# Layer 1's modulation beside the first mixer's attention, the second mixer's q products between the two norms, and roots with PSUM operands

## The chip, the cores and the metric

The kernel runs on one core of a Trainium2 chip. Its engines are TensorE (PE in the profile; PEld is its weight load), VectorE (DVE), ScalarE (ACT), GpSimd (POOL) and SyncE (SP), which issues most DMAs. The metric is the device time of one execution in microseconds, as the median of several runs.

## The reference

A two-layer diffusion trunk over 256 latent and 256 context tokens with D = 1024, in float32. Each layer takes six modulation vectors for each stream (latent and context) from a condition vector, runs a mixer and then a mixture of experts.

```python
for l in range(DEPTH):                       # two layers
    ml = split((silu(c)     @ ada_w[l] + ada_b[l]), 6)   # latent stream
    mc = split( silu(c_ctx) @ ada_w[l] + ada_b[l],  6)   # context stream
    nl = rmsnorm(hl, norm1_g[l]) * (1 + ml[1]) + ml[0]
    nc = rmsnorm(hc, norm1_g[l]) * (1 + mc[1]) + mc[0]
    if l % 2 == 0: yl, yc = conv_diffattn_mixer(nl, nc, ...)   # mixer 0
    else:          yl, yc = bigla_mixer(nl, nc, ...)           # mixer 1
    hl = hl + ml[2] * yl
    nl = rmsnorm(hl, norm2_g[l]) * (1 + ml[4]) + ml[3]
    y  = hier_moe(nl [and nc], ...)          # 32 experts, top 2 in the top group
    hl = hl + ml[5] * y                      # and hc likewise in layer 0
```

Mixer 0 is a convolution beside a differential attention (4 heads, two softmax maps each) with one joint output projection. Mixer 1 is a gated linear attention in both directions: products q, k, v and g of the normalized tokens, and a decay `log_sigmoid(a1 @ w_a2 + b_a2) / 16` from a low-rank gate.

## The kernel before

The program has four stages one after the other: mixer 0, MoE 0, mixer 1, MoE 1. The streams live in `H`, 128 tokens by 1024, blocks 0 and 1 latent, 2 and 3 context. Products in full precision are made of three (`mm3`): both operands are split into a rounded half `h` (by ScalarE) and the rest `l` (by GpSimd or VectorE), and PE takes h·h, h·l and l·h. `quarter` splits a quarter of a 1 MB weight tile so, on L371 (`wh`) and L372 (`wl`). Weight tiles come from one ring, `wt`, of four 1 MB buffers, and are loaded on SP's queue. The program is written in plain order; a scheduler then picks the order of each engine's instructions by a modelled time, so that a row's place on an engine is not that of its line. Every engine runs its own list strictly in order.

**Modulation.** `ada_steps(l, r)` computes the r-th pair of modulation vectors of layer l (r = 0: shift and scale of the first norm, 1: gate of the mixer and shift of the second, 2: the rest). It is a generator of eight steps; a step loads 1 MB of `ada_w` (L196) and multiplies it in four short products (L201). After the eighth it adds the bias (L210), for r other than 1 applies the norm's gain (L214), and for r other than 0 writes the rows to DRAM on GpSimd's queue. `ada_cols(1)` (L267) transposes (1,0) into columns for mixer 1.

**Mixer 0.** `attn_block(b, fill)` runs the attention of one block of 128 queries, four heads: QK products (L614), softmax, transposes of p (L634), P·V (L640), and calls `fill` after every head. For the latent blocks `fill_lat` makes one step of (1,0), eight in all; the four loads of w_out follow. For the context blocks `fill_ctx` makes a piece of `out_lat`, the latent half of the output projection: 96 products into `pj`, closed by `yt` (L710), from which the latent norm, route and modulate of MoE 0 start. The context half follows after the last block.

**Mixer 1.** It loads constants, sets `wf` to zero (L820) and loads the gate's weights into it by ten small loads (L823 to L827). `norm_mod_T` normalizes one stream: sums of squares (L325), reciprocal roots by an integer guess and two Newton steps (`rstd_of`, L280 to L286), `xn` (L328, L329), transposes (L335), then shift and scale into `xa` (L340) and its split into XH and XL (L341, L342). The code normalizes both streams, with the steps of (1,1) as filler whose tiles are mixer 1's own buffers, not yet in use (`S`, `sg`, `bT`, `attb`). Then come the gate: split weights `wv` (L879, L880) and `wa2h`, `wa2l` (L874, L875), products a1 and z (L895), and the decay L by Abs, Exp and Ln (L896 to L900). The q products (`lat_T`, L870) are written after it, then k, then the levels of the linear attention on VectorE, and the V projection, with (1,2) as filler.

Of the kernel before, what the change touches and what calls it, by code (L numbers as in the profile page):

```python
# [9 lines left out]
FT = mybir.dt.float32  # L10
FR = mybir.dt.float32r
BF = mybir.dt.bfloat16
I32 = mybir.dt.int32
U32 = mybir.dt.uint32
AF = mybir.ActivationFunctionType
# [4 lines left out]
D = 1024  # L20
# [60 lines left out]
def trunk_kernel(ctx: ExitStack, tc: tile.TileContext, A: dict, out: bass.AP):  # L81
# [7 lines left out]
    def pool(es, name, side):  # L89
        return es.enter_context(tc.tile_pool(name=name, bufs=1, side=side, reuse_waits="tile"))  # L90

    def pj(dt=FT):
        return psum.tile([128, 512], dt, name="pj", tag="pj", bufs=4)
# [6 lines left out]
    def wk(dt=FT):  # L100
        return wkp[0].tile([128, 512], dt, name="wk", tag="wk", bufs=2)
# [5 lines left out]
    def trps(dt=FT):  # L107
        return psum.tile([128, 512], dt, name="trps", tag="tr", bufs=2)
# [94 lines left out]
    def ada_steps(l, r, mpool, pool=None):  # L203

        m, bias, gn = ada_open(l, r, mpool)
        ps = trps() if (l, r) == (1, 2) else wk()
        for k in range(8):
            ada_k(ps, ada_tile(l, r, k, pool), k)
            if k == 7:
                nc.vector.tensor_add(m, bias, ps)  # L210
                if r != 1:
                    o = 64 if r == 0 else 0
                    v = m[o:o + 64]
                    nc.vector.scalar_tensor_tensor(v, v, 1.0, gn[o:o + 64], op0=OP.add, op1=OP.mult)  # L214
                if r:

                    ns = 2 - l
                    d = dram.tile([2, ns, D], FT, name=f"row{l}{r}", tag=f"row{l}{r}")
                    for h in range(2):
                        nc.gpsimd.dma_start(d[h].rearrange("s (g c) -> g s c", g=2), m[64 * h:64 * h + 64:16 * (2 // ns)])  # L220
                    rows[l, r] = d
            yield
# [39 lines left out]
    def ada_cols(l):  # L262

        t = const.tile([128, 2, 2, 4, 2], FT, name=f"cols{l}", tag=f"cols{l}")
        ps = trps()
        for i in range(4):
            nc.tensor.transpose(ps[:, i * 128:(i + 1) * 128], mods[l, 0][:, i * 128:(i + 1) * 128], ident)  # L267
        v = ps.rearrange("p (i g s r) -> p i g s r", i=4, g=4, s=2)[:, :, :, :, 0]
        for g in range(4):
            nc.vector.tensor_copy(t[:, g // 2, g % 2], v[:, :, g])  # L270
        return t.rearrange("p w g i s -> p w (g i) s")

    def rstd_of(dst, ss, n, pool, temps=None):

        c = 0.703952253
        k2 = (0.5 * c ** 3) ** 2
        sh = list(ss.shape)
        tag = f"rsq{sh[-1]}"
        w, t = temps or [pool.tile(sh, FT, name="rs" + i, tag=tag + i, bufs=2) for i in "wt"]
        nc.vector.tensor_scalar(w, ss, 1.0 / (n * k2), EPS / k2, op0=OP.mult, op1=OP.add)  # L280
        nc.vector.tensor_scalar(dst.bitcast(I32), w.bitcast(I32), 1, None, op0=OP.logical_shift_right)
        nc.vector.tensor_scalar(dst.bitcast(I32), dst.bitcast(I32), -1.0, float(0x5F1FFFF9), op0=OP.mult, op1=OP.add)
        for a in (2.38924456, 3 / c ** 2):
            nc.vector.tensor_mul(t, dst, dst)
            nc.vector.tensor_mul(t, t, w)
            nc.vector.scalar_tensor_tensor(dst, t, -a, dst, op0=OP.add, op1=OP.mult)  # L286

    def mm3(ps, st, mv, k0, k1):

        (sh, sl), (mh, ml) = st, mv  # L290
        nc.tensor.matmul(ps, sh, mh, start=k0, stop=False)  # L291
        nc.tensor.matmul(ps, sh, ml, start=False, stop=False)  # L292
        nc.tensor.matmul(ps, sl, mh, start=False, stop=k1)  # L293
# [24 lines left out]
    def norm_mod_T(pool, st, cols):  # L318

        ss = pool.tile([128, 2], FT, name="ss", tag="ss", bufs=2)  # L320
        rs = pool.tile([128, 2], FT, name="rs", tag="rs", bufs=2)
        xs = []
        for i in range(2):
            x = pool.tile([128, D], FT, name="xn", tag="xn", bufs=4)
            nc.scalar.activation(x, H[:, 2 * st + i], AF.Square, accum_out=ss[:, i:i + 1])  # L325
            xs.append(x)
        rstd_of(rs, ss, D, pool)
        nc.vector.tensor_scalar(xs[0], H[:, 2 * st], rs[:, 0:1], None, op0=OP.mult)  # L328
        nc.scalar.activation(xs[1], H[:, 2 * st + 1], AF.Copy, scale=rs[:, 1:2])  # L329
        t = slice(256 * st, 256 * st + 256)  # L330
        for kp in range(4):
            ps = trps()
            for j in range(4):
                k = 2 * kp + j // 2
                nc.tensor.transpose(ps[:, j * 128:(j + 1) * 128], xs[j % 2][:, k * 128:(k + 1) * 128], ident)  # L335
            for kk in range(2):
                k = 2 * kp + kk
                v = ps[:, kk * 256:kk * 256 + 256]
                a = pool.tile([128, 256], FT, name="xa", tag="xa", bufs=4)
                nc.vector.tensor_scalar(a, v, cols[:, 1, k, st:st + 1], cols[:, 0, k, st:st + 1], op0=OP.mult, op1=OP.add)  # L340
                nc.scalar.activation(XH[:, k, t], a, AF.Copy)  # L341
                (nc.gpsimd if kk else nc.vector).tensor_sub(XL[:, k, t], a, XH[:, k, t].bitcast(FT))  # L342
# [20 lines left out]
    def load_cols(src, pieces):  # L363
        return [load_half(src, pieces, hf) for hf in range(2)]

    def quarter(pool, ts, q, bufs, alt=False, dve=False):

        w = ts[q // 2][:, (q % 2) * 1024:(q % 2 + 1) * 1024]
        wh = pool.tile([128, 1024], FR, name="wh", tag="wsh", bufs=bufs)
        wl = pool.tile([128, 1024], FR, name="wl", tag="wsl", bufs=bufs)  # L370
        nc.scalar.activation(wh, w, AF.Copy)  # L371
        (nc.vector if dve or alt and q % 2 else nc.gpsimd).tensor_sub(wl, w, wh.bitcast(FT))  # L372
        return wh.rearrange("p (k n) -> p k n", k=2), wl.rearrange("p (k n) -> p k n", k=2)
# [25 lines left out]
    def mixer0():  # L399
        es = ExitStack()  # L400
        with es:
# [314 lines left out]
                    k = 2 * q + kk  # L716
                    mm3(ps, (ch[:, k, t], cl[:, k, t]), (w[0][:, kk], w[1][:, kk]), k == 0, k == 7)

            ad = ada_steps(1, 0, bp)
            ts = []  # L720

            def fill_lat(i):
                next(ad, None)

            def out_lat():
                for n in range(2):
# [19 lines left out]
                attn_block(b, fill_lat)  # L746
            for _ in ad:
                pass
            cols1[0] = ada_cols(1)
            ts += [load_cols(w, [(512 * n, 512)]) for n in range(2)]  # L750
            es6.close()
            es2.close()
# [31 lines left out]
    def mixer1():  # L784
        es = ExitStack()
        with es:
# [44 lines left out]
            def split2(x0, x1):  # L831

                hl = [xp.tile([128, 1024], FR, name="w" + t, tag="ws" + t, bufs=3) for t in "hl"]
                for i, x in enumerate((x0, x1)):
# [7 lines left out]
            rp = pool(es2, "raw1", "right")  # L842
            tsq = load_cols(w_in, [(0, 512)])


            free = [S.rearrange("p a h e -> p (a h e)"), sg.rearrange("p b c -> p (b c)"),
                    bT.rearrange("p a h t -> p (a h t)"), attb]

            fill = ada_steps(1, 1, mp, free[::-1])
            cols = cols1[0]  # L850
            for st in range(2):
                norm_mod_T(rp, st, cols)
            for _ in fill:
                pass
            es2.close()
            es4 = ExitStack()
            lp = pool(es4, "gl1", "right")
            L = lp.tile([128, 4, 2, 512], FT, name="L")
            vc = lp.tile([128, 2, D], FT, name="vc")

            def lat_T(w, pss, q):

                wh, wl = w
                for h in range(4):
                    for kk in range(2):
                        k = 2 * q + kk
                        o = pss[h // 2][:, 256 * (h % 2):256 * (h % 2) + 256]
                        a = slice(h * 128, (h + 1) * 128)
                        for i, (st, mv) in enumerate(((wh, xh), (wh, xl), (wl, xh))):
                            nc.tensor.matmul(o, st[:, kk, a], mv[:, k, :256], start=k == 0 and h % 2 == 0 and i == 0,  # L870
                                             stop=k == 7 and i == 2, skip_group_check=True)


            nc.scalar.activation(wa2s[0], wa2, AF.Copy)  # L874
# [25 lines left out]
                nc.vector.tensor_sub(L[:, bb[0]:bb[1] + 1], L[:, bb[0]:bb[1] + 1], E)  # L900


            pss = [pj(), pj()]
            for q in range(4):
                lat_T(quarter(xp, tsq, q, 3), pss, q)
            for i in range(2):
                nc.scalar.activation(qk[:, 0, 2 * i:2 * i + 2], pss[i].rearrange("p (h t) -> p h t", h=2), AF.Copy, scale=128 ** -0.5)
            ts = load_cols(w_in, [(512, 512)])
            pss = [pj(), pj()]
            pt = [pj(), pj()]  # L910
# [117 lines left out]
                nc.vector.tensor_copy(att[g:g + 32, :, g:g + 32], a32[g:g + 32])  # L1028


            fill = ada_steps(1, 2, mp, free[0:1])
            for n in range(2):
                _, pt = proj(xp, load_cols(w_in, [(1024 + 512 * n, 512)]), 3, toks=range(4), xh=xh, xl=xl, fill=fill)
                for i in range(2):
                    nc.scalar.activation(vc[:, i, n * 512:(n + 1) * 512], pt[2 + i], AF.Copy)
                    nc.vector.tensor_copy(V[:, i, n * 512:(n + 1) * 512], pt[i])
# [811 lines left out]
```

## Time and profile before

| | |
|---|---|
| median of 3 runs | 1535.17 us (1533.19 to 1537.72) |
| the profiled execution | 1534.12 us, span 1532.3 us, mean granted TensorE clock 0.944 |
| busy, of the span | PE 84%, PEld 43%, DVE 38%, ACT 24%, POOL 20% |
| HBM read | 495.68 MB, 324 GB/s over the span |
| MoE 0, MoE 1 | products from 357.9 us, and from about 1080 us |
| mixer 1's start | last product of MoE 0 (L1490) at 829.6 us |

The profile lists a row for each group of instructions: start, duration, engine, line, operation, output and inputs by their names (buffer numbers left out), shape; in square brackets the idle time of the engine just before it and what ended it. SPq is SP's queue of DMA issues. A row of the stretches view has the stretch, its length, the busy time and count of each engine, the granted clock, the mean busy share of the 16 DMA engines, and GB/s.

### The profile page before, as it was taken

The numbers are of one execution on the slowest core, as the hardware profiler recorded it, in microseconds if no ns is written. First come the engines' busy times: TensorE is split into PE (matmuls) and PEld (weight loads), VectorE is DVE, ScalarE is ACT, GpSimd is POOL, SyncE is SP. The second block draws the span as 40 slices with busy tenths as digits, with TensorE's granted clock in tenths as the row PEclk, the third lists the DMA queues.
The fourth block names the chain that finished last, engine by engine and source line by source line (L and its number), as shares of the span: only waits on it lengthen the run. The fifth ranks groups of instructions, "written<-read, shape, count | busy, mean of one in ns | idle before, by whom it ended". The sixth has DMA issues, their size and how long they took to land. (4 is left out here: it accounts for less than half of the span.)

```text
span 1532.3 us, 19018 instructions
## 1 busy us (share of the span) xinstructions
PE 1283.2 (84%) x7485; PEld 658.3 (43%) x7485; DVE 581.1 (38%) x1182; ACT 368.4 (24%) x700; POOL 300.5 (20%) x206
## 2 busy tenths in 40 slices
PE   5998978678789899999987999997965778767776
PEld 4665636564234345443422676675412212212211
DVE  4489895753002131231205556766202102202121
ACT  3245563451010101010102574444100000000000
POOL 1467601431001010100103443442000000000010
PEclk9999997898999999999998999998998899999989
DMA  9857261156999999999999623468799999999995
GB/s 317 287 204 256 108 220 48 68 212 277 421 422 424 422 422 423 412 422 423 423 424 357 226 92 133 166 224 352 301 427 427 426 426 427 427 427 426 427 426 250
DMA packets 100828, 498.10 MB, mean 325 GB/s; under 512 B 17605, under 2 KB 30248, under 8 KB 45948
## 3 DMA queue, kind: packets, MB, share of 16 engines
q1 hardware_dynamic: 96780, 490.37, 79.7%
q0 software_dynamic: 1680, 6.16, 1.2%
q8 instruction: 61, 1.00, 0.2%
q10 hardware_dynamic: 2272, 0.28, 0.2%
q14 instruction: 35, 0.29, 0.1%
HBM read 495.68 MB, written 1.10 MB: 324 GB/s over the span
## 5 line engine op out<-in xcount | busy, mean ns | idle before, releaser
L1553 PE MATMUL pj<-wx,xgT 128*32 128x512 f32 (+1 forms) x1496 | 313.9, 642 | 70.0 <-DMA wx<-in_moe_w_dram 70.0
L1553 PEld LDWEIGHTS pj<-wx,xgT 128*32 128x32 f32 (+1 forms) x1496 | 76.2, 120 | 256.6 <-DMA wx<-in_moe_w_dram 131.8
L1553 PE MATMUL pj<-wt,xgT 128*32 128x512 f32 (+1 forms) x704 | 160.1, 629 | 27.1 <-DMA wt<-in_moe_w_dram 23.4
L1453 DVE SCALAR_TENSOR_TENSOR s<-s,gc,pj 128x512 f32<-128x512 f32 x20 | 15.0, 748 | 428.8 <-PE pj L1553 374.4
L1562 PE MATMUL pj<-wx,hT 128*32 128x512 f32 (+1 forms) x792 | 167.4, 609 | 9.4 <-DMA wx<-in_moe_w_dram 5.3
L372 POOL TENSOR_TENSOR wl<-wt,wh 128x1024 fp32r<-128x1024 f32 x50 | 124.9, 2506 | 158.6 <-ACT wh L371 151.7
L291 PE MATMUL pj<-wh,XH 128*128 128x512 f32 x304 | 123.4, 416 | 18.8 <-ACT p L623 10.1
L292 PE MATMUL pj<-wl,XH 128*128 128x512 f32 x304 | 124.8, 410 | 1.4 <-POOL wl L372 1.4
L293 PE MATMUL pj<-wh,XL 128*128 128x512 f32 x304 | 122.8, 405 | 0.2
L1494 POOL TENSOR_TENSOR H<-H,sc 128x512 f32<-128x512 f32 x24 | 30.7, 1278 | 394.6 <-DVE sc L1493 394.6
L1481 POOL TENSOR_TENSOR H<-H,sc 128x512 f32<-128x512 f32 x16 | 20.4, 1275 | 446.3 <-DVE sc L1480 446.3
L371 ACT ACTIVATE wh<-wt 128x1024 fp32r<-128x1024 f32 x66 | 68.9, 1055 | 64.7 <-PE pj L293 44.3
L1553 PEld LDWEIGHTS pj<-wt,xgT 128*32 128x32 f32 (+1 forms) x704 | 37.9, 118 | 106.4 <-issue 59.2
L1562 PEld LDWEIGHTS pj<-wx,hT 128*32 128x32 f32 (+1 forms) x792 | 42.4, 114 | 94.1 <-issue 72.5
L291 PEld LDWEIGHTS pj<-wh,XH 128*128 128x128 f32 x304 | 58.9, 195 | 48.2 <-ACT p L623 11.6
L1452 ACT ACTIVATE s<-pj 128x512 f32<-128x512 f32 x20 | 12.0, 598 | 262.8 <-PE pj L1553 262.8
L1458 ACT ACTIVATE hT<-trps 128x512 f32<-128x512 f32 x20 | 11.9, 597 | 248.5 <-PE trps L1456 248.5
L545 DVE SCALAR_TENSOR_TENSOR wk<-hp,vt,wk 128x512 f32<-128x512 f32 x90 | 67.5, 750 | 1.7
L292 PEld LDWEIGHTS pj<-wl,XH 128*128 128x128 f32 x304 | 59.2, 195 | 17.6 <-issue 2.4
L293 PEld LDWEIGHTS pj<-wh,XL 128*128 128x128 f32 x304 | 59.1, 194 | 14.2 <-DVE XL L1096 1.3
L1562 PE MATMUL pj<-wt,hT 128*32 128x512 f32 (+1 forms) x280 | 54.6, 598 | 2.8 <-ACT hT L1458 2.8
L1388 PE MATMUL wk<-P,XH 128*128 128x256 f32 x192 | 52.2, 306 | 5.2 <-ACT xgT L1390 3.8
(468 smaller groups left out, 2020.1 us busy)
## 6 DMA issues: line engine op xcount, KB each, us to landing
wx<-in_moe_w_dram SPq DMA_DIRECT2D x266, 1024.0 KB, 19.6
wt<-in_moe_w_dram SPq DMA_DIRECT2D x107, 1024.0 KB, 19.6
wa<-in_ada_w_dram SPq DMA_DIRECT2D x16, 1024.0 KB, 4.8
wt<-in_gla_w_in_dram SPq DMA_DIRECT2D x12, 1024.0 KB, 8.0
H<-in_moe_w_dram SPq DMA_DIRECT2D x11, 1024.0 KB
S<-in_ada_w_dram SPq DMA_DIRECT2D x10, 1024.0 KB, 12.2
wt<-in_ada_w_dram SPq DMA_DIRECT2D x8, 1024.0 KB, 6.5
wt<-in_ab_w_in_dram SPq DMA_DIRECT2D x6, 1024.0 KB, 11.7
```

The lines of the kernel that those rows point to most:

```text
L291: nc.tensor.matmul(ps, sh, mh, start=k0, stop=False)
L292: nc.tensor.matmul(ps, sh, ml, start=False, stop=False)
L293: nc.tensor.matmul(ps, sl, mh, start=False, stop=k1)
L371: nc.scalar.activation(wh, w, AF.Copy)
L372: (nc.vector if dve or alt and q % 2 else nc.gpsimd).tensor_sub(wl, w, wh.bitcast(FT))
L545: e.scalar_tensor_tensor(av, hp[:, cb, :, t:t + 256], cw[:, t, cb:cb + 1], av, op0=OP.mult, op1=OP.add)
L1388: nc.tensor.matmul(ps[:, k], M['X'][h][:, k0 + k, b * 128:(b + 1) * 128], P[:, b], start=b == 0 and h == 0, stop=b == nb - 1 and h == 1)
L1453: nc.vector.scalar_tensor_tensor(s, s, gc, h3, op0=OP.mult, op1=OP.mult)
L1481: (nc.vector if hf else nc.gpsimd).tensor_add(H[:, b, c], H[:, b, c], t)
L1494: (nc.vector if hf else nc.gpsimd).tensor_add(H[:, b, c], H[:, b, c], t)
L1553: nc.tensor.matmul(ps[o:o + w], xgT[:, k, o:o + w], W[nm, x, k // 4][:, k % 4], start=k == 0, stop=k == 7)
L1562: nc.tensor.matmul(ys[hf][o:o + w], hT[:, k, o:o + w], W["2", x, k // 2][:, k % 2, hf * 512:(hf + 1) * 512], start=k == 0, stop=k == 3)
```

## The change

1. In mixer 0, a generator `early` makes the steps of (1,0), then the columns of (1,0), then the steps of (1,1) and of (1,2): 24 steps in place of 8. `fill_lat` makes three of them per head. All 24 loads use the `wt` ring.
2. In mixer 1 the filler steps and their borrowed buffers are gone.
3. In mixer 1 the q products are written between the norm of stream 0 and that of stream 1, ahead of the gate.
4. `norm_mod_T` uses a new root, `rstd_free`: its guess and its square are held in a PSUM bank (`wk`), and the square is made by ScalarE.
5. The bank of (1,2)'s sums is a `wk` one like the others.

```diff
-        ps = trps() if (l, r) == (1, 2) else wk()
+        ps = wk()
...
+    def rstd_free(dst, ss, n, pool):
+
+        c = 0.703952253
+        k2 = (0.5 * c ** 3) ** 2
+        m = ss.shape[-1]
+        w = pool.tile(list(ss.shape), FT, name="rsw", tag=f"rsq{m}w", bufs=2)
+        b = wk()
+        d0, t = b[:, 0:m], b[:, m:2 * m]
+        nc.vector.tensor_scalar(w, ss, 1.0 / (n * k2), EPS / k2, op0=OP.mult, op1=OP.add)
+        nc.vector.tensor_scalar(d0.bitcast(I32), w.bitcast(I32), 1, None, op0=OP.logical_shift_right)
+        nc.vector.tensor_scalar(dst.bitcast(I32), d0.bitcast(I32), -1.0, float(0x5F1FFFF9), op0=OP.mult, op1=OP.add)
+        for a in (2.38924456, 3 / c ** 2):
+            nc.scalar.activation(t, dst, AF.Square)
+            nc.vector.tensor_mul(t, t, w)
+            nc.vector.scalar_tensor_tensor(dst, t, -a, dst, op0=OP.add, op1=OP.mult)
...
-        rstd_of(rs, ss, D, pool)
+        rstd_free(rs, ss, D, pool)
...
-            ad = ada_steps(1, 0, bp)
+            def early():
+
+                yield from ada_steps(1, 0, bp)
+                cols1[0] = ada_cols(1)
+                for r in (1, 2):
+                    yield from ada_steps(1, r, bp)
+            ad = early()
...
             def fill_lat(i):
-                next(ad, None)
+                for _ in range(3):
+                    next(ad, None)
...
-            cols1[0] = ada_cols(1)
             ts += [load_cols(w, [(512 * n, 512)]) for n in range(2)]
...
-            free = [S.rearrange("p a h e -> p (a h e)"), sg.rearrange("p b c -> p (b c)"),
-                    bT.rearrange("p a h t -> p (a h t)"), attb]
-
-            fill = ada_steps(1, 1, mp, free[::-1])
             cols = cols1[0]
-            for st in range(2):
-                norm_mod_T(rp, st, cols)
-            for _ in fill:
-                pass
...
+            norm_mod_T(rp, 0, cols)
             def lat_T(w, pss, q):
...
+            pss = [pj(), pj()]
+            for q in range(4):
+                lat_T(quarter(xp, tsq, q, 3), pss, q)
+            for i in range(2):
+                nc.scalar.activation(qk[:, 0, 2 * i:2 * i + 2], pss[i].rearrange("p (h t) -> p h t", h=2), AF.Copy, scale=128 ** -0.5)
+            norm_mod_T(rp, 1, cols)
...
-            fill = ada_steps(1, 2, mp, free[0:1])
             for n in range(2):
-                _, pt = proj(xp, load_cols(w_in, [(1024 + 512 * n, 512)]), 3, toks=range(4), xh=xh, xl=xl, fill=fill)
+                _, pt = proj(xp, load_cols(w_in, [(1024 + 512 * n, 512)]), 3, toks=range(4), xh=xh, xl=xl)
```

The lines behind the root shift by 15 or 16, and in mixer 1 by 21 or 22: mm3 is L307 to L309, QK L630, p's transposes L650, P·V L656, `yt` L726, the squares' sums L341, `xn` L344 and L345, `xa` L356, XH L357, `wh` and `wl` L387 and L388, `wf`'s loads L845 to L849, `wa2h` L895, `wv` L900.

On PE, in mixer 0, the first product of `out_lat` (`pj_1770<-wh_...`, from w_out) before, with the eighth and last modulation step (`wt_2062`) ahead of it:

```order
L640 MATMUL wk_1772<-V_593,at_1896 128x128 x4
L201 MATMUL wk_1805<-wt_2062,st32_81 32x512 x4
L614 MATMUL pj_1768<-kT_592,qT_591 128x512
L614 MATMUL pj_1769<-kT_592,qT_591 128x512
L614 MATMUL pj_1770<-kT_592,qT_591 128x512
L614 MATMUL pj_1771<-kT_592,qT_591 128x512
L614 MATMUL pj_1768<-kT_592,qT_591 128x256 x2
L614 MATMUL pj_1769<-kT_592,qT_591 128x256 x2
L291 MATMUL pj_1770<-wh_2198,XH_75 128x512
L292 MATMUL pj_1770<-wl_2199,XH_75 128x512
```

And the same place after the change, with the last seven of the 24 steps (`wk_2089` collects (1,2)):

```order
L201 MATMUL wk_2089<-wt_2096,st32_81 32x512 x4
L201 MATMUL wk_2089<-wt_2128,st32_81 32x512 x4
L630 MATMUL pj_1768<-kT_592,qT_591 128x256 x2
L685 MATMUL trps_2219<-cst_71,o4_2195 128x128 x4
L630 MATMUL pj_1769<-kT_592,qT_591 128x256 x2
L201 MATMUL wk_2089<-wt_2134,st32_81 32x512 x4
L201 MATMUL wk_2089<-wt_2140,st32_81 32x512 x4
L201 MATMUL wk_2089<-wt_2172,st32_81 32x512 x4
L201 MATMUL wk_2089<-wt_2178,st32_81 32x512 x4
L201 MATMUL wk_2089<-wt_2184,st32_81 32x512 x4
L307 MATMUL pj_1770<-wh_2313,XH_75 128x512
```

The attention of the second latent block and QK products of the first context block, of which a part stood behind `out_lat`'s first products, now stand ahead of them, between the steps.

On ACT, at mixer 1's start before (`xn` of the two streams, XH of stream 0, then the gate's weights):

```order
L329 ACTIVATE xn_6097<-H_66,rs_6094 128x1024
L329 ACTIVATE xn_6168<-H_66,rs_6165 128x1024
L341 ACTIVATE XH_75<-xa_6117 128x256
L341 ACTIVATE XH_75<-xa_6121 128x256
L341 ACTIVATE XH_75<-xa_6130 128x256
L341 ACTIVATE XH_75<-xa_6134 128x256
L341 ACTIVATE XH_75<-xa_6143 128x256
L341 ACTIVATE XH_75<-xa_6147 128x256
L341 ACTIVATE XH_75<-xa_6156 128x256
L879 ACTIVATE wv_6291<-wf_6072 128x16x32 x2
L874 ACTIVATE wa2h_6057<-wf_6072 128x512
```

And after (`wk_6215` holds stream 0's square, `wk_6402` stream 1's):

```order
L300 ACTIVATE wk_6215<-rs_6209 128x2
L900 ACTIVATE wv_6474<-wf_6187 128x16x32 x2
L895 ACTIVATE wa2h_6172<-wf_6187 128x512
L300 ACTIVATE wk_6215<-rs_6209 128x2
L300 ACTIVATE wk_6402<-rs_6396 128x2
L345 ACTIVATE xn_6212<-H_66,rs_6209 128x1024
L300 ACTIVATE wk_6402<-rs_6396 128x2
L345 ACTIVATE xn_6399<-H_66,rs_6396 128x1024
L357 ACTIVATE XH_75<-xa_6232 128x256
```

The casts of the gate's weights have moved from behind stream 0's XH to between its two Newton steps. On VectorE `wv`'s and `wa2l`'s subtractions (L901, L896) have moved to the same place. On SP, the first load of MoE 1's weights has moved to just ahead of `wf`'s ten loads, where four loads of (1,1) stood; and on PE the first z product of the gate stands behind 150 products of L879 and 48 of `mm3`, in place of 86 and 24.

More of the change, by code (lines that the diff above doesn't have):

```diff
@@ L843, in mixer1 @@
             tsq = load_cols(w_in, [(0, 512)])
-            free = [S.rearrange("p a h e -> p (a h e)"), sg.rearrange("p b c -> p (b c)"),
-                    bT.rearrange("p a h t -> p (a h t)"), attb]
-            fill = ada_steps(1, 1, mp, free[::-1])
             cols = cols1[0]
-            for st in range(2):
-                norm_mod_T(rp, st, cols)
-            for _ in fill:
-                pass
[L855 to L859, printed above, removed]
+            norm_mod_T(rp, 0, cols)
             def lat_T(w, pss, q):
@@ L871, in lat_T @@
                                              stop=k == 7 and i == 2, skip_group_check=True)
+            pss = [pj(), pj()]
[4 more added lines that the diff above has]
+            norm_mod_T(rp, 1, cols)
+            es2.close()
+            es4 = ExitStack()
+            lp = pool(es4, "gl1", "right")
+            L = lp.tile([128, 4, 2, 512], FT, name="L")
+            vc = lp.tile([128, 2, D], FT, name="vc")
             nc.scalar.activation(wa2s[0], wa2, AF.Copy)
@@ L900, in mixer1 @@
                 nc.vector.tensor_sub(L[:, bb[0]:bb[1] + 1], L[:, bb[0]:bb[1] + 1], E)
[L903 to L907, printed above, removed]
             ts = load_cols(w_in, [(512, 512)])
```

## The prediction

> **What bounds the kernel now.** I read the page's time slices and its chain first, to find the stages that the end hangs on, then the stretches around them.
>
> ```profile
> DMA  9857261156999999999999623468799999999995
> GB/s 317 287 204 256 108 220 48 68 212 277 421 422 424 422 422 423 412 422 423 423 424 357 226 92 133 166 224 352 301 427 427 426 426 427 427 427 426 427 426 250
> DMA 22%; PE 1%; DVE 0%; SPq 0%; issue 0%; ACT 0%; DVEq 0%
> DMA wx<-in_moe_w_dram 15%; DMA wt<-in_moe_w_dram 6%; PE pj L1553 1%; PE pj L1562 0%; DVE sc L1480 0%; DVE H L1481 0%; SPq L1507 0%; PE wk L1476 0%; PE trps L1456 0%; DVE s L1453 0%; ACT XH L1465 0%; ACT hT L1458 0%; PE trps L1417 0%; DVEq L1480 0%; DVEq L1453 0%
> ```
>
> A slice is 38.3 us. Two plateaus of about 424 GB/s are the expert weights of the two MoEs, and the chain that ended last is made of their loads. The change touches neither. What counts is when each plateau may start:
>
> ```profile
> 350.00:360.00 10.00, 10.00 (x63) 8.41 (x61) 2.62 (x28) 1.97 (x4) 0.00 (x0) 0.75 0.36 125
> 1080.00:1090.00 10.00, 10.00 (x84) 2.98 (x80) 0.63 (x4) 2.26 (x3) 0.00 (x0) 0.90 0.51 186
> ```
>
> In both rows (PE, PEld, DVE, ACT, POOL busy; granted clock; DMA share; GB/s) the DMAs idle half the time just ahead of a MoE: its free buffers are full and wait to be used. A mixer that ends later therefore moves its plateau by as much. The change in time is the shift of mixer 0's end plus the change in mixer 1's length.
>
> **Mixer 0: 16 more modulation steps.** One step is a 1 MB load and four short products.
>
> ```profile
> 198.00:218.00 20.00, 7.69 (x64) 1.67 (x64) 1.00 0.71 280
> 832.00:845.00 13.00, 4.93 (x24) 0.58 (x24) 0.66 0.66 233
> 845.00:875.00 30.00, 7.02 (x40) 0.96 (x40) 0.92 0.63 237
> 900.00:985.00 85.00, 8.55 (x64) 1.32 (x64) 0.98 0.44 149
> ```
>
> These are L201 alone (PE busy and records, eight to a step). Mixer 0's eight steps cost 7.69 us, 0.96 each; 16 more are 15.4 us of PE. The same 16 leave mixer 1 (the other rows: 3, 5 and 8 of them).
>
> ```profile
> 200.00:210.00 10.00, 9.31 (x61) 4.19 (x61) 9.96 (x25) 6.45 (x13) 0.00 (x0) 1.00 0.61 232
> 210.00:220.00 10.00, 8.73 (x64) 4.26 (x63) 9.97 (x19) 9.83 (x20) 0.00 (x0) 1.00 1.02 409
> 220.00:230.00 10.00, 4.63 (x10) 2.07 (x10) 9.63 (x27) 5.17 (x9) 0.00 (x0) 0.76 0.74 201
> 230.00:240.00 10.00, 9.44 (x41) 7.10 (x41) 4.47 (x15) 2.88 (x7) 0.00 (x0) 0.72 0.01 2
> 250.00:260.00 10.00, 6.51 (x22) 4.34 (x22) 7.98 (x29) 4.84 (x17) 0.62 (x2) 0.80 0.00 0
> 211.74 5.79 SPq L359 DMA_DIRECT2D wt<-in_ab_w_out_dram  x4
> 231.87 0.80 PE L291 MATMUL pj<-wh,XH 128*128 128x512 f32 x1 [0.22 <-ACT p L623]
> 276.24 0.69 DVE L710 TENSOR_TENSOR yt<-pj,g 128x512 f32<-128x512 f32 x1 [1.90 <-PE pj L293]
> L291 PE MATMUL pj<-wh,XH 128*128 128x512 f32 x14 | 6.7, 477 | 0.6 <-ACT XH L672 0.3 <-ACT p L623 0.2
> ```
>
> The attention leaves PE 0.69, 1.27, 5.37, 0.56 and 3.49 us idle in the five stretches to 260, 11.4 us, and the DMAs move next to nothing in the rows at 230 and 250. So there is room; the question is whether the order lets the steps use it. The 24 loads share the four buffers of the `wt` ring, and w_out's four loads, on the same queue and ring and issued from 211.74 on before, now stand behind all of them. On PE all 24 steps stand ahead of the first product of `out_lat`; before, that product ran at 231.87.
>
> Step 13 stands about where that product stood. With five more steps ahead of it (4.8 us) it comes at about 237, and its buffer can take load 17 only then. A load of 1.05 MB at the 409 GB/s of the second row is 2.56 us; eight more (17 to 24) from 238 on take 20.5, so step 24 runs near 259, the first load of w_out lands near 261, and with its halves split `out_lat` starts near 263, 31 us later than now. It isn't delayed by 31 us at its end: before, only about 42 of its 96 products (14 on L291, one of `mm3`'s three lines, from 231.5 to 261: the last row) had run by 261, in between the attention of the second latent block and the first of the context, and that attention now runs while the steps wait. What is left is 96 products in one piece. At full clock one takes 0.23 us, twice the 0.11 of the half as wide ones quoted further below: 22.4 us, and some 1.5 more at the lower clock that follows idle time (0.72 in the row at 230). Its end, from the last product to `yt`, goes from 276.2 to about 287: **+11 us**. After it, nothing is saved:
>
> ```profile
> 290.00:300.00 10.00, 1.00 (x3) 0.25 (x2) 9.89 (x19) 4.37 (x3) 0.00 (x0) 0.51 0.00 0
> ```
>
> VectorE's chain of route and norm, which starts from `yt`, keeps the last attention block waiting here, and moves with it. The bounds: +4 if every step falls into idle time (15.4 - 11.4), +16 if none does. The two row stores on POOL's queue and mod11's and mod12's additions are small beside this and stand in DVE's order between pieces of the attention; at 0.7 us for an addition of this size (the `yt` row) I put them at nothing, hidden by the same waits, and 2 us if they aren't. The transposes of `cols1` only move, and the other bank of (1,2) costs nothing.
>
> **Mixer 1's start: a stall goes, a wait comes.**
>
> ```profile
> 834.67 0.75 DVE L328 TENSOR_SCALAR xn<-H,rs 128x1024 f32<-128x1024 f32 x1
> 835.54 2.23 DVE L282 TENSOR_SCALAR rs<-rs 128x2 int32<-128x2 int32 x1
> 837.80 2.26 DVE L284 TENSOR_TENSOR rst<-rs 128x2 f32<-128x2 f32 x1
> 840.10 2.27 DVE L285 TENSOR_TENSOR rst<-rst,rsw 128x2 f32<-128x2 f32 x1
> 842.40 0.16 DVE L286 SCALAR_TENSOR_TENSOR rs<-rst,rs 128x2 f32<-128x2 f32 x1
> 843.85 1.89 DVE L340 TENSOR_SCALAR xa<-trps,cols 128x256 f32<-128x256 f32 x4
> 835.37 6.97 POOL L372 TENSOR_TENSOR wl<-wt,wh 128x1024 fp32r<-128x1024 f32 x3 [1.80 <-ACT wh L371]
> ```
>
> Three operations on 128x2 numbers, 0.16 us where nothing is beside them, take 2.2 to 2.3 each while POOL makes `wl`: 6.3 us lost, and stream 0's `xa` stands behind them. The new root keeps its temporaries in PSUM and squares on ScalarE, which removes up to these 6.3 us. [...]
>
> But the order puts something in its place. On ScalarE the two casts of `wv` and the one of `wa2h` (L879 and L874; L900 and L895 in the changed kernel) now stand ahead of the second Newton step's Square for stream 0, and on VectorE the two subtractions behind them likewise. They wait for the ten `wf` loads:
>
> ```profile
> 831.64 0.95 POOL L820 MEMSET wf<- 128x1024 f32 x1
> 832.62 7.00 SPq L823 DMA_DIRECT2D wf<-in_gla_w_in_dram  x2
> 839.67 3.67 SPq L826 DMA_DIRECT2D wf<-in_gla_w_a_dram  x1
> 845.76 0.27 SPq L827 DMA_DIRECT2D wf<-in_gla_b_a_dram  x1
> wf<-in_gla_w_a_dram SPq DMA_DIRECT2D x4, 32.0 KB, 1.7
> 850.03 0.62 ACT L874 ACTIVATE wa2h<-wf 128x512 fp32r<-128x512 f32 x1
> ```
>
> Before, the last was issued at 845.8 and landed about 847.7 (1.7 us). Now no modulation loads are ahead of them, but one 1 MB load of MoE 1's weights is (2.56 us). I take a landing at 845; the bounds are 847.7 (nothing gained) and 839, where the loads are issued in 0.3 us each as the last one was. From the landing: `wa2h` 0.62, Square and two root operations 0.5, `xn` 0.75, the root and `xn` of stream 1 that stand ahead in DVE's order 1.5 to 2: `xa` at about 849, 5 us later than 843.85 (bounds -1 and +8). I take 5, since the nearest row, the issue at 839.67, still lasts 3.67 with nothing but small pieces ahead of it.
>
> **Mixer 1 beyond.** Five steps (7.02 us) leave a stretch in which PE is full; but the gate's products (L895 before) now stand behind 64 more products of L870, 0.11 us apart, and 24 of `mm3`, 12.9 us:
>
> ```profile
> 850.00:860.00 10.00, 10.00 (x74) 7.72 (x71) 7.05 (x12) 5.48 (x11) 7.74 (x6) 1.00 1.02 421
> 899.61 0.28 PE L870 MATMUL pj<-XL,wh 128*128 128x256 f32 x1
> 899.73 0.28 PE L870 MATMUL pj<-XH,wl 128*128 128x256 f32 x1
> L895 PE MATMUL wk<-wa2h,a x8: 492/496/501, 872.7 to 897.0; 64*128 64x512 f32 x8
> 903.04 2.29 DVE L900 TENSOR_TENSOR L<-L,attb 128x2048 f32<-128x2048 f32 x1 [2.30 <-ACT attb L899]
> 910.00:920.00 10.00, 8.55 (x50) 5.48 (x52) 10.00 (x8) 6.99 (x9) 7.18 (x3) 1.00 0.47 147
> 950.00:960.00 10.00, 10.00 (x57) 7.58 (x56) 4.85 (x6) 4.58 (x7) 3.21 (x2) 1.00 0.38 138
> ```
>
> The first gate product moves from 872.7 by +5 - 7 + 12.9 to about 884. Then the chain of Abs, Exp and Ln is denser than before, since its later products waited on PE (872.7 to 897.0 for eight), and the decay's last subtraction starts at about 904.5 instead of 903: +1.5 us. The stretch after it is VectorE's (10.00 at 910) and keeps its length. In the V products PE is full (10.00), and six of the eight steps of (1,2) leave it: -6.4 us. Mixer 1: **-5 us**, with bounds -12 (loads at 839, gate chain early) and +1 (loads at 847.7, and half of the V gain taken by VectorE). That the q products are written between the norms moves nothing by itself: they started ahead of the second stream's transposes already.
>
> **The sum.** 11 - 5 = +6 on the profiled execution's 1534.1 us gives 1540.1. It lies 1.05 under the median of 1535.17, so the median should come to about **1541 us**.
>
> **Rivals.** *The steps cost their full time* (+16, and mixer 1 no shorter): 1551. For it: out_lat's loads last in the queue; against: 11.4 us of idle PE.
> *The loads of `wf` come early*: if they land by 839, the root's gain is paid, mixer 1 gives about -11 and the two parts cancel: 1535. For it: before, 4 MB stood ahead of them on the queue, now 1. [...]
> *Faster*: out_lat's thin work fills in. Place: PE from 231 to 276. If the loads keep the ring turning so that w_out's first load lands by about 256, the 24 steps cost only what idle time doesn't take, +4, and with early `wf` loads (-11) the sum is -7: 1528. For it: DMAs free from 230 on; against: step 13's place behind the attention.
> *The change doesn't do what it says*: of the move between the norms that is so, and it is in the sum; the steps and the roots move in the order as stated.
>
> **Chances.** Forecast 0.42, full cost 0.16, early `wf` 0.22, faster 0.20. Within 0.3%, 4.6 us, is what a measurement here can't tell from no change. Of the forecast's 0.42 I count 0.34 above 1539.8 and 0.08 below it. Slower: 0.34 + 0.16 = 0.50; same: 0.08 + 0.22 = 0.30; faster 0.20. The range runs from just under the faster case to just over the full cost, 1527 to 1552.
>
> **What would show it.** Right: `out_lat`'s first product near 263, `yt` near 287, MoE 0's first product near 369 (357.9 now); in mixer 1 root operations of 0.2 us, `wa2h`'s cast after idle time that a `wf` load ended, the first `xa` about 17 us after the start of `wf`'s memset (12.2 now), and no L201 after 300. Wrong: `yt` below 282 or above 291; `wf` landed before the roots ask; a V stretch as long as before.

## The result and the profile after

The changed kernel takes 1553.15 us (median of 4 runs, 1550.88 to 1555.19) against 1535.29 before: a ratio of 1.0107, 95% interval 1.0087 to 1.0126. It is slower, as forecast, but by 18 us and not by 6. The median lies 1 us above the range's end of 1552; by the ratio, on the 1535.17 us that the forecast started from, it would be 1551.6.

The stages of the profiled executions, before and after (in us; the difference is that of the time since the mark above, or since the start):

| | before | changed | difference |
|---|---|---|---|
| last `yt` of `out_lat` | 277.71 | 300.59 | +22.9 |
| first product of MoE 0 | 357.88 | 377.71 | -3.1 |
| end of its last scatter product | 829.99 | 852.54 | +2.7 (MoE 0) |
| first `xa` of mixer 1 | 843.85 | 867.13 | +0.7 |
| first gate product z | 872.69 | 901.32 | +5.4 |
| last subtraction of the decay L | 903.04 | 928.78 | -2.9 |
| first product of MoE 1 | 1078.51 | 1097.30 | -7.0 |
| end of the span | 1532.30 | 1551.90 | +0.8 (MoE 1) |

Mixer 0 ends 19.8 us later (forecast +11), MoE 0 takes 2.7 more (not forecast), mixer 1 is 3.8 shorter (forecast 5).

The page's slices of the changed kernel: the gap of the DMAs that stood at 48 and 68 GB/s is filled now, and the plateaus are as high as before.

```profile
DMA  9867279435999999999998402267799999999995
GB/s 318 289 210 257 84 281 331 145 134 211 422 423 421 423 423 422 415 394 424 422 423 360 116 27 80 85 200 307 277 426 427 425 427 427 426 428 425 428 426 249
```

Stretches in mixer 0 (PE, PEld, DVE, ACT, POOL busy; clock; DMA share; GB/s), then steps and first product of `out_lat` on PE, the last `yt`, and SP's queue:

```profile
220.00:230.00 10.00, 8.14 (x46) 3.19 (x46) 7.01 (x28) 5.86 (x14) 0.00 (x0) 1.00 1.02 344
230.00:240.00 10.00, 5.04 (x26) 2.52 (x28) 3.33 (x11) 1.71 (x4) 0.00 (x0) 0.70 0.84 290
260.00:270.00 10.00, 6.79 (x38) 0.76 (x32) 0.04 (x1) 0.00 (x0) 0.00 (x0) 0.67 0.93 337
270.00:280.00 10.00, 8.21 (x24) 5.61 (x21) 5.73 (x6) 4.12 (x4) 5.93 (x9) 0.59 1.09 386
...
235.98 1.93 PE L201 MATMUL wk<-wt,st 128*32 128x512 f32 x8 [4.96 <-DMA wt<-in_ada_w_dram]
268.73 1.93 PE L201 MATMUL wk<-wt,st 128*32 128x512 f32 x8 [1.81 <-DMA wt<-in_ada_w_dram]
272.41 1.22 PE L307 MATMUL pj<-wh,XH 128*128 128x512 f32 x2 [1.75 <-ACT wh L387]
300.59 0.69 DVE L726 TENSOR_TENSOR yt<-pj,g 128x512 f32<-128x512 f32 x1 [0.54 <-PE pj L309]
...
202.67 13.66 SPq L196 DMA_DIRECT2D wt<-in_ada_w_dram  x8
217.65 0.58 SPq L163 DMA_DIRECT2D bias<-in_ada_b_dram  x1
219.60 28.44 SPq L196 DMA_DIRECT2D wt<-in_ada_w_dram  x8
262.98 8.11 SPq L375 DMA_DIRECT2D wt<-in_ab_w_out_dram  x4
```

PE is all but alone from 260 to 270 and waits for loads; the last step runs at 268.7, and w_out's loads are issued from 263 on. Once `out_lat` has started, PE is full, at first at half the clock:

```profile
274.00:278.00 4.00, 4.00 (x10) 3.17 (x10) 2.17 (x2) 0.92 (x1) 3.42 (x6) 0.50 1.14 349
280.00:300.00 20.00, 19.70 (x100) 15.36 (x100) 11.38 (x14) 7.68 (x9) 10.01 (x6) 1.00 0.29 63
```

What PE waited for in this part (us, times, longest), before, after, and with 16 steps (an experiment below), from 196 us to 262, 272 and 262:

```profile
PE pj L614 <- ACT p L623: 10.5, 7, 3.3
```

```profile
PE wk L201 <- DMA wt<-in_ada_w_dram: 8.6, 5, 5.0
PE pj L630 <- ACT p L639: 3.4, 5, 1.1
```

```profile
PE pj L614 <- ACT p L623: 3.1, 4, 1.3
```

The wait for the softmax is what steps can fill. Both kernels with more steps fill some 7 us of it; with 24 a wait for loads takes its place.

Mixer 1's start in the changed kernel:

```profile
854.82 0.95 POOL L842 MEMSET wf<- 128x1024 f32 x1
855.79 1.00 SPq L845 DMA_DIRECT2D wf<-in_gla_w_in_dram  x2
860.86 0.28 SPq L849 DMA_DIRECT2D wf<-in_gla_b_a_dram  x1
859.93 1.15 ACT L900 ACTIVATE wv<-wf 128x512 fp32r<-128x512 f32 x2 [0.80 <-DMA wf<-in_gla_w_in_dram]
862.43 0.63 ACT L895 ACTIVATE wa2h<-wf 128x512 fp32r<-128x512 f32 x1 [1.36 <-DMA wf<-in_gla_b_a_dram]
860.96 2.89 DVE L901 TENSOR_TENSOR wv<-wf,wv 128x512 fp32r<-128x512 f32 x2
867.13 1.89 DVE L356 TENSOR_SCALAR xa<-trps,cols 128x256 f32<-128x256 f32 x4
L916 PE MATMUL wk<-wa2h,a x8: 492/494/792, 901.3 to 920.5; 64*128 64x512 f32 x8
```

The casts end their wait on loads of `wf`, as foreseen; but these loads take 5.3 us to issue, against 13.4 before, and `wa2h`'s cast starts 7.6 us after the memset's start. `xa` is 12.3 us behind the memset's start, as before (12.2).

### The profile page after: what moved, and what is told of

Its sections match the earlier page's. It is cut to its first block, busy times and chain, and to the rows that moved or that the text cites. A ratio compares the mean times of both kernels' runs of the same rounds, so it can differ in the third digit from the quotient of the medians.

```text
span 1551.9 us, 19026 instructions
## 1 busy us (share of the span) xinstructions
PE 1291.6 (83%) x7485; PEld 660.6 (43%) x7485; DVE 580.0 (37%) x1178; ACT 368.7 (24%) x704; POOL 305.2 (20%) x206
## 5 line engine op out<-in xcount | busy, mean ns | idle before, releaser
L1577 PE MATMUL pj<-wx,hT 128*32 128x512 f32 (+1 forms) x792 | 170.8, 615 | 9.3 <-DMA wx<-in_moe_w_dram 5.1
L388 POOL TENSOR_TENSOR wl<-wt,wh 128x1024 fp32r<-128x1024 f32 x50 | 126.4, 2536 | 143.9 <-ACT wh L387 140.7
L307 PE MATMUL pj<-wh,XH 128*128 128x512 f32 x304 | 122.5, 415 | 20.0 <-ACT p L639 10.6
L309 PE MATMUL pj<-wh,XL 128*128 128x512 f32 x304 | 122.9, 405 | 0.2
L387 ACT ACTIVATE wh<-wt 128x1024 fp32r<-128x1024 f32 x66 | 68.9, 1055 | 74.1 <-PE pj L309 41.5
L307 PEld LDWEIGHTS pj<-wh,XH 128*128 128x128 f32 x304 | 58.8, 195 | 46.9 <-ACT p L639 11.0
L1467 ACT ACTIVATE s<-pj 128x512 f32<-128x512 f32 x20 | 11.9, 597 | 256.7 <-PE pj L1568 256.7
L1473 ACT ACTIVATE hT<-trps 128x512 f32<-128x512 f32 x20 | 11.9, 597 | 251.1 <-PE trps L1471 250.9
L309 PEld LDWEIGHTS pj<-wh,XL 128*128 128x128 f32 x304 | 58.7, 193 | 14.6 <-DVE XL L1111 1.3
## 6 DMA issues: line engine op xcount, KB each, us to landing
wx<-in_moe_w_dram SPq DMA_DIRECT2D x266, 1024.0 KB, 19.6
```

Source lines behind the costliest of these rows:

```text
L1577: nc.tensor.matmul(ys[hf][o:o + w], hT[:, k, o:o + w], W["2", x, k // 2][:, k % 2, hf * 512:(hf + 1) * 512], start=k == 0, stop=k == 3)
```

## The experiments

All times are medians beside runs of the kernel before on the same chip. MoE 0 and mixer 1 are the stages of the table above; before, MoE 0 starts at 357.9 us and takes 472.1, and mixer 1, from the last scatter product to MoE 1's first product, takes 248.5. The first three columns are of one profiled execution each.

Mixer 0 is the same program before and in e1, e6, e7 and e12, and MoE 0 starts there at 357.5 to 362.6 us. Counted from the attention's first QK product it starts after 167.7 to 168.6 us in all five, so that the 4.7 us of e12 arose ahead of the attention. Counted so, e3 is 3.0 us behind the kernel before, the changed kernel 20.1 behind and e5 5.4 ahead.

| kernel | MoE 0 starts | MoE 0 | mixer 1 | median | ratio (95%) |
|---|---|---|---|---|---|
| changed | 377.7 | 474.8 | 244.8 | 1553.15 | 1.0107 (1.0087-1.0126) |
| e1_no_ada | 358.4 | 472.1 | 255.3 | 1541.65 | 1.0036 (1.0026-1.0046) |
| e2_ada_only | 377.7 | 472.9 | 238.8 | 1545.21 | 1.0056 (1.0037-1.0075) |
| e3_one_load | 361.3 | 472.3 | 247.4 | 1535.53 | 0.9996 (0.9987-1.0006) |
| e4_16_steps | 354.9 | 472.1 | 300.8 | 1585.98 | 1.0323 (1.0304-1.0341) |
| **e5_16_alone** | 352.4 | 474.4 | 240.2 | **1524.37** | **0.9927 (0.9914-0.9940)** |
| e6_root_only | 357.5 | 474.9 | 248.2 | 1536.38 | 1.0012 (1.0000-1.0023) |
| e7_q_only | 358.0 | 471.8 | 250.3 | 1540.81 | 1.0029 (1.0014-1.0044) |
| e8_16_root | 352.5 | 474.2 | 244.3 | 1530.42 | 0.9956 (0.9938-0.9974) |
| e9_start12 | 351.5 | 473.7 | 245.6 | 1528.61 | 0.9947 (0.9927-0.9966) |
| e10_20_loads | 366.5 | 477.6 | 248.5 | 1546.73 | 1.0062 (1.0037-1.0086) |
| e11_poolq | 372.3 | 474.5 | 244.9 | 1549.01 | 1.0080 (1.0055-1.0104) |
| e12_xn_on_act | 362.6 | 471.9 | 248.1 | 1534.68 | 0.9987 (0.9969-1.0005) |

**Which part loses: e1, e2.** One undoes the move of the modulation in the changed kernel, the other makes that move alone in the kernel before.

```diff
 e1, from the changed kernel:
-        ps = wk()
+        ps = trps() if (l, r) == (1, 2) else wk()
...
-            ad = early()
+            ad = ada_steps(1, 0, bp)
...
+            fill = ada_steps(1, 1, mp, free[::-1])
             norm_mod_T(rp, 0, cols)
+            for _ in fill:
+                pass
...
+            fill = ada_steps(1, 2, mp, free[0:1])
```

> Modulation back in mixer 1 ((1,1) between the norms, (1,2) in the V projection); the q products between the norms and the new root stay. Theory 1 (nearly all of the loss is mixer 0's, through the loads): MoE 0's first product back at 358 us (378 in the changed kernel), whole time 1531 to 1540. Theory 2 (the new order of mixer 1 loses as well: its first gate product came 6 us late): over 1540.

> The kernel before with the moved modulation alone (24 steps in mixer 0, none in mixer 1; old root, old place of the q products). Both theories: MoE 0's first product at 376 to 380 us. Theory 1: mixer 1 gains most of its 15 us of steps, 8 or more, so 1541 to 1547, below the changed kernel's 1553. Theory 2 says the same of this run, and at least 5 us less than the changed kernel. If instead taking the steps out of mixer 1 is worth little by itself: 1550 or more.

Measured: 1541.65 and 1545.21. Each part loses by itself, 0.36% and 0.56%; their sum, 0.92%, lies within the interval of the whole. The move costs mixer 0 its 19.8 us and gives mixer 1 9.7 back (248.5 to 238.8). The other two edits take 6.0 of these away again (244.8), and 6.8 where the modulation stays (255.3). So theory 2, that the new order of mixer 1 loses as well, holds beside theory 1.

**What sets mixer 0's pace: e3, e10, e11.** Two kernels keep all 24 steps' products and drop loads; the third keeps the loads and takes the bias and gain loads off SP's queue.

```diff
 e3:
-            ada_k(ps, ada_tile(l, r, k, pool), k)
+            if k == 0 or (l, r) not in ((1, 1), (1, 2)):
+                aw = ada_tile(l, r, k, pool)
+            ada_k(ps, aw, k)
 e10:
+            if k % 2 == 0 or (l, r) != (1, 2):
 e11:
-        m, bias, gn = ada_open(l, r, mpool)
+        m, bias, gn = ada_open(l, r, mpool, nc.gpsimd if (l, r) in ((1, 1), (1, 2)) else None)
```

> The changed kernel with one load for all eight steps of (1,1), and one for (1,2), 14 MB less; all products stay. It leaves out the other seven eighths of these weights. If the loads set the pace in mixer 0: out_lat's first product before 255 us (272 in the changed kernel), MoE 0's first product at 361 to 366, whole time 1537 to 1543. If the PE time of the steps (15 us) sets it: MoE 0 at 373 or later, 1548 or more.

> The changed kernel with every load of (1,2) used for two steps: 20 loads in mixer 0 in place of 24, all products kept. It leaves out half of the weights of (1,2). If the loads set the pace up to the last step, each saves its 2.9 us: MoE 0's first product at 364 to 368 (377.7), whole time 1538 to 1543. If the loads matter only through the queue's blocking by the bias loads: 374 or later.

> The changed kernel with the bias and gain loads of (1,1) and (1,2) on GpSimd's queue, so that the weight loads behind them on SP's queue don't wait for the sum before. If these waits are what empties the DMAs (0.84 and 0.94 busy between 230 and 250): out_lat 3 to 6 us earlier, MoE 0's first product at 372 to 375. If it is the bytes: 376 to 379, and 1551 to 1555 as the changed kernel.

The first product of `out_lat` in e3, e10 and e11 (272.41 in the changed kernel):

```profile
246.25 0.50 PE L309 MATMUL pj<-wh,XH 128*128 128x512 f32 x1
```

```profile
262.21 0.73 PE L309 MATMUL pj<-wh,XH 128*128 128x512 f32 x2 [1.78 <-ACT wh L389]
```

```profile
268.13 0.74 PE L307 MATMUL pj<-wh,XH 128*128 128x512 f32 x2 [1.88 <-ACT wh L387]
```

With 10 loads MoE 0 starts at 361.3, with 20 at 366.5, with 24 at 377.7. All 24 steps' products, with ten loads, cost 3.4 us, near the forecast's lower bound of 4. The step from 10 loads to 20 costs 5.2 us, and that from 20 to 24 costs 11.2, 2.8 a load. So it is the loads that delay mixer 0, the last of them most. The total of e3 lies 1.5 us below its expectation. That of e10 lies above: its MoE 0 took 477.6 us in the profiled execution, and mixer 1 3.7 more than the changed kernel's. The queue's waits are a part: without them `out_lat` starts 4.3 us earlier and MoE 0 5.4. Stretches of e11, and its bias and gain loads on GpSimd's queue:

```profile
220.00:230.00 10.00, 8.86 (x52) 3.81 (x48) 5.67 (x23) 4.24 (x10) 0.67 (x1) 0.92 1.03 339
230.00:240.00 10.00, 7.93 (x60) 4.46 (x56) 6.59 (x20) 5.28 (x12) 0.00 (x0) 1.00 1.00 349
240.00:250.00 10.00, 9.21 (x64) 5.12 (x60) 4.97 (x16) 3.73 (x11) 1.77 (x3) 0.94 1.01 421
250.00:260.00 10.00, 7.48 (x44) 2.56 (x44) 5.17 (x17) 2.98 (x9) 0.00 (x0) 0.84 0.99 334
...
218.72 0.73 POOL L163 DMA_DIRECT2D bias<-in_ada_b_dram  x1 [35.55 <-DVE mod L210]
245.90 0.71 POOL L163 DMA_DIRECT2D bias<-in_ada_b_dram  x1
```

The two bias loads landed 11.6 and 14.8 us after their issue. The DMAs are full in all four rows. The trace's packets of these loads (each row of a load goes to 32 partitions) start from 222.7 to 237.1 us and from 250.2 to 255.4, and none between: in the three rows with such packets the DMAs move 334 to 349 GB/s, and 421 in the one without. That is a coincidence of rows; it was not tried by itself.

**How many steps fit: e4, e5.** Both move (1,1) alone, two steps a head. In e4 (1,2) goes back to the V projection of the changed kernel; e5 is the kernel before with this one edit.

```diff
 e5, from the kernel before (e4 has the same generator, and (1,2) as in e1 but in a wk bank):
-            ad = ada_steps(1, 0, bp)
+            def early():
+
+                yield from ada_steps(1, 0, bp)
+                cols1[0] = ada_cols(1)
+                for r in (1,):
+                    yield from ada_steps(1, r, bp)
+            ad = early()
...
-                next(ad, None)
+                for _ in range(2):
+                    next(ad, None)
...
-            fill = ada_steps(1, 1, mp, free[::-1])
```

> The changed kernel with (1,1) alone moved to mixer 0 (16 steps, two per head); (1,2) back in the V projection. If the loads set the pace: eight loads at 2.9 us and a bias load fewer, so MoE 0's first product some 15 to 18 us earlier than in the changed kernel's 378, at 360 to 364, and 4 to 6 us given back in mixer 1: 1540 to 1545. If PE time sets it: MoE 0 at 370, 1548 to 1552.

> The kernel before with (1,1) alone moved to mixer 0 (16 steps, two per head); (1,2) stays in the V projection with its own bank; old root, old place of the q products. Theory 1 (the loads set mixer 0's pace, and up to about 16 steps they end before w_out is asked for): MoE 0's first product at 354 to 359 us as with 16 steps before, mixer 1 shorter by the five steps in its full stretch, 4 to 7 us: 1526 to 1531, faster than before. If the steps cost mixer 0 in proportion (a third to a half of 19.8 us): 1537 or more.

e5 is the fastest of all, 1524.37 us, 0.73% under the kernel before: mixer 0 ends 5.5 us earlier than before, mixer 1 is 8.4 shorter. All three are better than the case that it was to show (354 to 359 us, 4 to 7, 1526 to 1531). Its `out_lat` starts 11.9 us later than before and ends 2.7 earlier:

```profile
243.77 0.74 PE L291 MATMUL pj<-wh,XH 128*128 128x512 f32 x2
```

```profile
275.04 0.69 DVE L710 TENSOR_TENSOR yt<-pj,g 128x512 f32<-128x512 f32 x1 [0.54 <-PE pj L293]
```

So a late `out_lat` costs nothing at first, since what stood between its products has run already; in the changed kernel it starts 28.6 us later than in e5 and ends 25.6 later. e4 has much the same mixer 0 (354.9, earlier than either of its cases) and loses 52 us in mixer 1, of which 34 are one row of PE's waits:

```profile
PE wk L201 <- DMA S<-in_ada_w_dram: 34.1, 7, 5.0
```

There the scheduler put all eight steps of (1,2) behind the V products in one piece, and each but the first waits 5 us for the one buffer's next load. In the kernel before and in e5 they stand among the products, and so they do in e1, which has the new root and the q products' new place, and in e8, which has the new root and 16 steps. All these keep (1,2)'s sums in the other PSUM bank; e4 alone does not. That points to the bank, but it was not tried by itself.

**The root and the q products: e6, e7, e8, e12.** The new root alone, the q products' new place alone, the root in the 16-step kernel, and the root alone with both `xn` made by ScalarE.

```diff
 e6, e8:
-        rstd_of(rs, ss, D, pool)
+        rstd_free(rs, ss, D, pool)
 e7: as e1, with
-        rstd_free(rs, ss, D, pool)
+        rstd_of(rs, ss, D, pool)
 e12: as e6, with
-        nc.vector.tensor_scalar(xs[0], H[:, 2 * st], rs[:, 0:1], None, op0=OP.mult)
+        nc.scalar.activation(xs[0], H[:, 2 * st], AF.Copy, scale=rs[:, 0:1])
```

> The kernel before with the new root alone. If the root is what it says and nothing takes its place: first xa 6 us earlier after the last product of MoE 0 (13.9 us before), 1529 to 1533. If a wait for the gate's weights takes its place: first xa at 12 to 15, 1534 to 1538. If the root is the part of mixer 1 that loses: 1539 or more.

> The kernel before with the q products written between the norms, old root, all modulation where it was. If this is the part of mixer 1 that loses, because the gate's first product then stands behind more of the k products and projection (38 to 40 us after the first xa, 28.8 before): 1540 to 1545, as the run without moved modulation. If not: 1533 to 1537.

> The 16-step kernel with the new root added. Theory 1 with a root that pays here (no modulation loads stand ahead of the gate's weights): 2 to 6 us under the 16-step kernel. If the root only trades its stall for the wait: within 1.5 us of it.

> The root-only kernel with both scaled copies xn of a stream made by ScalarE, so that VectorE has no operation from SBUF to SBUF between the root and xa while GpSimd makes wl. There, VectorE's two xn took 5.1 us in place of 1.5 and ended with GpSimd's work; first xa 13.3 us after the last product of MoE 0. If the stall that the root no longer has was handed on to xn in this way: first xa at 10.5 to 11.5. If something else held it: 13 or more. The whole time stays within 4 us of the root-only kernel either way, since ScalarE's casts of the gate's weights, which wait for wf's loads, stand ahead of XH.

e6 gains nothing (1.0012; first `xa` 13.3 us after the last scatter product, 13.9 before). These are the numbers of its second case, but not by a wait for the gate's weights. VectorE and PE there:

```profile
840.71 5.09 DVE L344 TENSOR_SCALAR xn<-H,rs 128x1024 f32<-128x1024 f32 x2
```

```profile
840.73 1.94 PE L201 MATMUL wk<-attb,st 128*32 128x512 f32 x8 [8.30 <-DVE rs L302]
```

The root's operations take 0.16 us each, as planned. But its Squares stand behind three casts of `wh` on ScalarE (2.93 us), so it ends at 840.7; the first modulation step, which filled this time before (833.15), waits 8.3 us for the root's last operation, which reads the PSUM bank that the root has taken from the ring of the step's own; and the two `xn`, 0.75 us each elsewhere, take 5.09 while GpSimd makes `wl` (837.80 to 845.24). The stall went to the next operation from SBUF to SBUF. In the changed kernel it is `wv`'s subtraction, 2.89 us for two of 0.68 (the row of L901 above). e12 was to show this by itself and doesn't: stream 0's `xn` was done at 845, but its transposes stood on PE behind two modulation steps, of which the first had waited 8.31 us for the root's bank, and the first `xa` came at 14.5, in the case that something else held it; the whole time stayed with the kernel before. So the handing on of the stall rests on the durations alone.

e8 is about 6 us slower than e5 (1530.42, 1524.37), outside both of its cases. The root is not seen to cost this. In the profiled executions, 4.0 us apart, the decay's last subtraction comes 68.2 us after the last scatter product, against 67.9 in e5; mixer 1's 4.1 us more arise after 980, where PE waits for one of GpSimd's splits. GpSimd, VectorE and PE in e8, then VectorE in e5, where GpSimd's split took 2.55 us:

```profile
980.77 5.16 POOL L388 TENSOR_TENSOR wl<-wt,wh 128x1024 fp32r<-128x1024 f32 x1
981.30 0.67 DVE L1027 TENSOR_TENSOR Ev<-bT 128x512 f32<-128x512 f32 x1
985.98 0.51 PE L308 MATMUL pj<-wl,XH 128*128 128x512 f32 x1 [2.49 <-POOL wl L388]
```

```profile
981.09 2.56 DVE L1011 TENSOR_TENSOR Ev<-bT 128x512 f32<-128x512 f32 x1
```

The same two operations meet in both; in e5 VectorE's is the long one, in e8 GpSimd's, and there PE needs it. Why it went the other way stays open.

e7 loses 0.29%, not to be told apart from the 0.36% with the root. Its first gate product comes 49.4 us after the last scatter product (42.7 before, 39.5 in e2, 48.8 in the changed kernel), and 34.1 after the first `xa`, less than the 38 to 40 expected. Its profiled execution, of 1536.81 us, was among the faster ones: mixer 1 is only 1.8 us longer in it.

```profile
L916 PE MATMUL wk<-wa2h,a x8: 492/494/496, 879.2 to 900.2; 64*128 64x512 f32 x8
```

**A further step: e9.** From e5, with (1,2) taken to mixer 1's start, where (1,1) stood before, and its sums in a `wk` bank.

```diff
...
+            fill = ada_steps(1, 2, mp, free[::-1])
...
-            fill = ada_steps(1, 2, mp, free[0:1])
```

> The 16-step kernel with the eight steps of (1,2) taken from the V projection to where (1,1) stood in the kernel before: mixer 1's start, tiles in four buffers that are not yet in use. If idle time of PE there takes three of them and the loads are prefetched: mixer 1 2 to 4 us shorter than in the 16-step kernel, 1520 to 1523. If the loads delay the gate's weights and the first xa: 1524 to 1530.

1528.61: not better than e5. The second case's time came out, and mixer 1 took 245.6 us against 240.2. The first `xa` was not delayed (14.5 us after the last scatter product, 15.1 in e5), but the gate's weights were: `wv`'s casts start at 844.35, at 834.95 in e5, and the decay's last subtraction comes 3.3 us later.

## Why the prediction was right or wrong

- *MoEs bound by their loads, and a shift of mixer 0 passed on in full.* Right: MoE 0 starts 19.8 us later and takes about as long. That the span grew by nearly the same, 19.6, is chance, since the other stages' +2.7, -3.8 and +0.8 almost cancel. (Of the two rows read for this, the second begins after MoE 1's first product, at 1078.51, not ahead of it.) The 2.7 us more of MoE 0 were not foreseen. In one stretch the DMAs fell to 0.97:

```profile
660.00:700.00 40.00, 39.04 (x289) 17.14 (x286) 6.87 (x17) 7.01 (x12) 1.17 (x1) 1.00 0.97 398
```

  e6, whose MoE 0 starts as before, has such a stretch too (0.94 and 377 GB/s from 620 to 660) and 474.9 us; over all runs MoE 0 took 471.8 to 477.6. It doesn't follow the change; its cause stays open.
- *Step 13 at 237.* It ran at 235.98. *Step 24 near 259*: 268.7. This is the step that failed: step 24 came 32.7 us after step 13, where the forecast had 22. The term was eight loads of 2.56 us at 409 GB/s; the DMAs moved 290 to 344 GB/s from 220 to 270. SP's queue stood behind the bias and gain loads, which wait for the sum before (e11: 4.3 us of `out_lat`'s start), and full DMAs moved less (344 GB/s at a share of 1.02 from 220 to 230, 329 at 1.00 from 250 to 260). The rate had been read in a stretch without such a load, and the queue's waits had no term in the sum.
- *`out_lat`: 24 us in one piece.* 28.2 (272.4 to 300.6): the clock was 0.50 from 274 to 278, and products started 0.43 us apart until then and 0.23 us apart after it, so that half clock cost some 3 us, twice the 1.5 foreseen. PE did not wait for w_out's later halves; transposes that stood between the products and a 0.30 us wait for a `yt` make up most of the rest. With start and length, +11 became +23 at the last `yt` (277.71 before; the 276.24 of the prediction is the one ahead of it), and after it 3.1 us were saved where the text said nothing is.
- *The mechanism of mixer 0* (loads through the ring, w_out behind them) is shown by e3 and e10, and so is the bound of +4: 3.4 without the loads. The upper bound of +16 was wrong: it counted PE time only, though the text's own pace was the loads'. That the whole time came out near the rival of full cost, 1551, is chance: the steps' PE time did not cause it.
- *A stall goes, a wait comes.* Right in kind. In size, `xa` came 0.7 us later, not 5: with no modulation loads ahead, the `wf` loads were issued in 5.3 us. In e9, with four such loads ahead again, it was 13.3 (829.16 to 842.46). Over all fourteen kernels it was 12.8 to 14.2 us in the six with four modulation loads issued shortly ahead, and 4.1 to 5.3 in the eight with one 1 MB load there. So what the prediction had put down to small pieces goes with the big loads ahead of them.
- *The rival of early `wf` loads.* Its condition was met and its price wasn't. `wa2h`'s cast started 7.6 us after the memset's start, where a landing at 839 is 7.4; but `xa` stood behind `wv`'s subtraction and came as late as before, and mixer 1 was 3.8 us shorter, not 11.
- *Where the stall went.* In the changed kernel the root's operations with a PSUM operand, from 860.34 to 860.82, took 0.15 to 0.16 us each beside `wl` (855.73 to 862.69), and its one from SBUF to SBUF 1.32 (859.11); before, three took 2.2 to 2.3. That PSUM operands and a square on ScalarE would do this was the author's estimate: no row of the prediction shows it, and it was not tried apart from the move of the square. By the durations the stall went to VectorE's next operations: `xn`, 5.09 us for two in e6, and `wv`'s subtraction, 2.89 for two in the changed kernel. The prediction looked at the root alone and not at the operations that come next.
- *The gate.* First product +11.3 us with `xa` at +5, so +7 with the `xa` that came; measured 48.8 after the last scatter product against 42.7, +6.1. The decay's last subtraction: +1.5 forecast, +3.2 measured (both from the last scatter product). The stretch between the two was taken too short: 20.5 us forecast, 27.5 measured, 30.4 before, since the later products waited for ScalarE's Abs and Exp (6.4 us in four waits). The V stretch: -6.4 forecast, -7.0. Mixer 1: -5 forecast, -3.8. This is near in part by luck, since the first gate product came 5.2 us earlier than forecast and the chain behind it took 7 longer.
- *"That the q products are written between the norms moves nothing by itself."* Wrong: e7 loses 0.29%, and its first gate product comes 6.7 us later. The prediction had seen the gate's new place and put it down to no edit.

## What to carry to other kernels

Here idle PE time took fill work for free only while the fill's loads kept ahead: eight more steps made mixer 0 5.5 us shorter, and eight beyond them made it 25.3 longer again (MoE 0 starts at 352.4 with 16 steps, at 377.7 with 24), because the output weights stood behind their loads in ring and queue. Count the fill's loads against the time until the next load that someone waits for, with the small loads in the same queue that wait for results. Here a stall beside GpSimd's work went, by the durations, to the next VectorE operation from SBUF to SBUF (two `xn` in e6, 5.09 us; 0.75 each elsewhere), so look at the whole chain beside that work before moving one operation out of it.

## What was not expected of the hardware

Full DMAs were not always as fast: in e11 421 GB/s in one stretch, at a busy share of 1.01, and 334 to 349 in its neighbours, at 0.99 to 1.03, in which packets of loads that copy one row to 32 partitions were under way. Small strided loads were issued slowly behind big ones: the ten `wf` loads took 12.8 to 14.2 us to issue with four 1 MB loads shortly ahead and 4.1 to 5.3 with one. Neither was tried by itself.
